# A second buffer for the gate's copy out of PSUM, and the decay exponentials with the token's own sum taken off by the matmul

## The chip, the cores and the metric

The kernel runs on one core of a Trainium2 chip. The metric is the device time of one execution in microseconds (us). The five engines of a core are named as in the profile: PE (TensorE, matmuls; PEld is its weight load), DVE (VectorE), ACT (ScalarE), POOL (GpSimd) and SP (SyncE, which here only issues DMAs).

## The reference

One layer of a bidirectional encoder in 32-bit floating point, on 1280 tokens (a prompt of 1024 and a sample of 256) of width 1024. A normed input is projected to three groups of heads that run side by side: six heads of a gated delta rule (DeltaNet) in both directions, six retention heads in both directions, and four heads of windowed attention. Each group's output is multiplied by a gate, and two dense stages follow. What the change touches, cut to its core:

```python
decay = jnp.cumsum(to_chunks(g, CHUNK), axis=-1)            # CHUNK = 64
gamma = jnp.exp(jnp.where(incl, decay[..., :, None] - decay[..., None, :], -jnp.inf))
a_mat = jnp.einsum('nbhcd,nbhsd->nbhcs', k_beta, k) * gamma
t_mat = jnp.where(strict, a_mat, 0.0) + jnp.eye(CHUNK, dtype=q.dtype)
sol = lax.linalg.triangular_solve(t_mat, rhs, left_side=True, lower=True, unit_diagonal=True)
qk = jnp.einsum('nbhcd,nbhsd->nbhcs', q, k) * gamma
...
o_a = (rms_norm(o_fwd + o_bwd, dn_norm_g) * jax.nn.silu(heads(a_gate, A_HEADS))).reshape(b, t, A_WIDTH)
o_b = head_layer_norm(r, ret_norm_g.astype(f32)) * jax.nn.silu(b_gate)
o_c = window_attention(...) * jax.nn.silu(c_gate)
```

`gamma` is the exponential of a difference of two running sums: that of the column's token and that of the row's own token. There is one 64x64 matrix of it per head, chunk and direction. `silu(gate)` is the gate times its sigmoid.

## The kernel before, in words

**Dense products.** Thirty products of the form "128 output columns times 1280 tokens" make up most of PE's work. To keep precision, weight and input are each split into a high and a low part, and a product is three matmuls for each of eight slices of the width, in three blocks of tokens (512, 512, 256). Their accumulators come from the PSUM tag "mm". Each block is then taken out of PSUM by an evacuation.

**Stages.** Input, norm and transposes come first; then nine products with a convolution each (34 to 213 us in the trace of before); among them `beta_alpha` (L317 to L371), which computes the running sums of the decays, writes their high and low parts to DRAM (`DRD`, L371, a POOL DMA) and keeps the negative of each token's own sum in `negd` (L364). Then comes `prep_stream` (L572 to L624; 213 to 345 us), woven with the ten products of `PP`: "cq0", "cq1", 6, 7, 3, "ck", "cv", 4, 0, 5. The products named by numbers are gates. After it come the second inversion, the attention, the scan over chunks (`join`, `step`), retention, and from about 850 us the two final dense stages. Products `PB` (gates 1 and 2, then "q0") run beside the attention.

**A gate's evacuation** (`evg`, L464 to L475): ACT copies the block out of PSUM into `zt` (tile "sz", L468); `sigmoid` makes `sg` from it with three activations (Exp L100, Ln L101, Exp L102); DVE multiplies `sg` by `zt`; for gates 0 to 5 an SP DMA writes the result to DRAM (`GD`, L472). `sz` and `sg` have one buffer each (SGB = 1). So a copy waits for the multiply of the block before, and L100 waits for the DMA of the block before.

**Preparing a block** (`prep_stream`): blocks of 128 tokens run from the last to the first, each in two directions d = 0, 1; one block in one direction is called a round here, 20 in all. Per block PE makes the grams ("sa") and transposes k into `kt` (PSUM tag "tr"), which ACT copies out (`kc`, L588). Per round POOL loads four rows of the running sums into DJ[d] (L591, two DMAs; one buffer per direction), PE makes two products `pd` of 128x384 (PSUM tag "sb") with DJ[d] as the moving and SD[0] or SD[1] as the stationary side, and ACT takes the exponential into `ge`: for the first `pd` six activations of 128x64 (L598), one for each head and chunk, because each has its own bias column of `negd`; for the second one of 128x384 (L601). The rows 64 to 127 of the first product bring in the mask. ACT then fills a column of `at` (L607; two buffers, AB = 2), DVE makes the products of grams and `ge` into `at` and `l2`, POOL copies `elc` (L616), and SP issues their DMAs (L618 to L621).

**Inversion and join.** `invert(1)` runs behind the fifth block, `invert(0)` behind the tenth: DVE inverts 32x32 pieces in steps, and the result goes through DRAM (`yd`, then `yn`) to `join`, whose matmuls on PE precede the scan.

**Order.** The generators are woven by due times written in the code (T_PREP and others), and a scheduler with a simulated timeline then sets each engine's order, with priority for weight splits and evacuations. Each engine works through its own list in order: what stands behind a waiting instruction waits too.

## Time and profile before

| what | value |
|---|---|
| median of 3 runs | 1095.5 us (1093.81 to 1100.48) |
| the profiled execution, its own time | 1098.55 us |
| its span | 1096.7 us |
| mean granted clock of PE in it | 0.959 |

The profile belongs to one execution, whose own time is 3.05 us above the median and 1.85 us above its span. Times inside it are microseconds from the start of the span. A line number behind an engine's name is that of the kernel before; a helper records all DVE products under L89 and all matmuls under L86, so that those are told apart by their tiles: `mm<-xh,whi` is a dense product, `sb<-dj,sd` a decay product, `sz` and `sg` are the gate's tiles, `ge` the exponentials, `at` and `l` what goes to the inversion and the scan.

### The profile page before, as it was taken

The numbers are of one execution on the slowest core, as the hardware profiler recorded it, in microseconds if no ns is written. First come the engines' busy times: TensorE is split into PE (matmuls) and PEld (weight loads), VectorE is DVE, ScalarE is ACT, GpSimd is POOL, SyncE is SP. The second block draws the span as 40 slices with busy tenths as digits, with TensorE's granted clock in tenths as the row PEclk, the third lists the DMA queues.
The fourth block names the chain that finished last, engine by engine and source line by source line (L and its number), as shares of the span: only waits on it lengthen the run. The fifth ranks groups of instructions, "written<-read, shape, count | busy, mean of one in ns | idle before, by whom it ended". The sixth has DMA issues, their size and how long they took to land.

```text
span 1096.7 us, 23201 instructions
## 1 busy us (share of the span) xinstructions
PE 1023.4 (93%) x8909; PEld 868.3 (79%) x8909; DVE 640.9 (58%) x1371; ACT 521.8 (48%) x1265; POOL 271.3 (25%) x430
## 2 busy tenths in 40 slices
PE   5999999999897889999998899999799999999996
PEld 4768878887775767878776777777579999999996
DVE  6666677477799679845565755575883123311125
ACT  7576776577456445344444322323342013455554
POOL 2001000022123021222233325544442211233421
PEclk9999999999999889999999799969889999999999
DMA  8112112367866363463464334554372432101003
GB/s 259 35 44 68 44 39 61 75 169 199 194 176 186 84 159 86 111 136 86 111 167 120 108 92 122 138 152 115 112 244 86 144 112 78 39 1 49 11 39 154
DMA packets 201415, 120.70 MB, mean 110 GB/s; under 512 B 105042, under 2 KB 186234, under 8 KB 201306
## 3 DMA queue, kind: packets, MB, share of 16 engines
q1 hardware_dynamic: 196410, 118.97, 39.8%
q8 instruction: 70, 1.15, 0.4%
q0 software_dynamic: 4896, 0.27, 0.4%
q14 instruction: 39, 0.32, 0.1%
HBM read 76.26 MB, written 42.91 MB: 109 GB/s over the span
## 4 chain that ended last, share of the span: by engine, by line
PE 63%; DVE 14%; DMA 10%; issue 4%; ACT 3%; SPq 2%; POOL 2%; DVEq 0%; ACTq 0%; POOLq 0%
PE mm L86 36%; PE sa L86 14%; PE sb L86 6%; PE tr L86 3%; DMA ad<-at 3%; DVE ot L89 3%; DVE l L89 1%; DMA yd<-ot 1%; SPq L618 1%; DMA gd<-sg 1%; DVE ot L966 1%; DMA vt<-vtd 1%; DMA yn<-yd 1%; DMA xt<-in_x_prompt 1%; PE tr L848 1%
## 5 line engine op out<-in xcount | busy, mean ns | idle before, releaser
L86 PE MATMUL mm<-xh,whi 128*128 128x512 f32 x720 | 270.0, 375 | 13.9 <-ACT sz L468 11.5
L86 PE MATMUL mm<-xl,whi 128*128 128x512 f32 x720 | 265.3, 369 | 0.0
L86 PE MATMUL mm<-xh,wlo 128*128 128x512 f32 x720 | 264.2, 367 | 0.0
L86 PEld LDWEIGHTS mm<-xh,whi 128*128 128x128 f32 x720 | 139.5, 194 | 40.0 <-ACT sz L468 13.5
L86 PEld LDWEIGHTS mm<-xh,wlo 128*128 128x128 f32 x720 | 139.6, 194 | 21.6 <-issue 0.5
L86 PEld LDWEIGHTS mm<-xl,whi 128*128 128x128 f32 x720 | 140.1, 195 | 20.5 <-issue 0.7
L89 DVE TENSOR_TENSOR ot<-ot 128x1284 f32<-128x1284 f32 (+16 forms) x131 | 88.0, 672 | 20.0 <-ACT ot L102 15.1
L86 PE MATMUL sa<-whi,xh 128*128 128x256 f32 x320 | 91.1, 285 | 0.0
L86 PE MATMUL sa<-whi,xl 128*128 128x256 f32 x320 | 90.4, 282 | 0.4 <-DVE xl L89 0.4
L86 PE MATMUL mm<-whi,xh 128*128 128x256 f32 x320 | 90.7, 284 | 0.0
L86 PE MATMUL mm<-whi,xl 128*128 128x256 f32 x320 | 90.4, 283 | 0.1
L86 PE MATMUL mm<-wlo,xh 128*128 128x256 f32 x320 | 90.3, 282 | 0.0
L86 PE MATMUL sa<-wlo,xh 128*128 128x256 f32 x320 | 90.1, 281 | 0.0
L89 DVE TENSOR_TENSOR sgm<-sb,sgm 128x256 f32<-128x256 f32 x40 | 17.0, 424 | 94.0 <-ACT sgm L102 73.8
L86 PEld LDWEIGHTS sa<-whi,xl 128*128 128x128 f32 x320 | 60.2, 188 | 0.8 <-DVE xl L89 0.6
L86 PEld LDWEIGHTS mm<-whi,xh 128*128 128x128 f32 x320 | 60.4, 189 | 0.4 <-issue 0.2
L86 PEld LDWEIGHTS sa<-whi,xh 128*128 128x128 f32 x320 | 60.2, 188 | 0.5 <-issue 0.3
L86 PEld LDWEIGHTS mm<-whi,xl 128*128 128x128 f32 x320 | 60.2, 188 | 0.5 <-DVE xl L89 0.3
L86 PEld LDWEIGHTS mm<-wlo,xh 128*128 128x128 f32 x320 | 60.3, 188 | 0.2 <-issue 0.2
L86 PEld LDWEIGHTS sa<-wlo,xh 128*128 128x128 f32 x320 | 60.2, 188 | 0.0
L525 DVE SCALAR_TENSOR_TENSOR ot<-ot,cols 128x1284 f32<-128x1284 f32 x36 | 55.9, 1552 | 0.6
L86 PE MATMUL sa<-sv,l 128*64 128x64 f32 (+1 forms) x912 | 47.3, 240 | 7.8 <-DVE sv L730 4.6
(294 smaller groups left out, 2097.3 us busy)
## 6 DMA issues: line engine op xcount, KB each, us to landing
raw<-in_w_in SPq DMA_DIRECT2D x28, 512.0 KB, 3.8
l2d<-l SPq DMA_DIRECT2D x20, 576.0 KB, 3.6
l<-l2d SPq DMA_DIRECT2D x40, 288.0 KB, 3.2
xt<-in_x_prompt SPq DMA_DIRECT2D x8, 512.0 KB, 6.9
x<-in_x_prompt SPq DMA_DIRECT2D x32, 128.0 KB, 2.7
raw<-in_w_pg SPq DMA_DIRECT2D x4, 1024.0 KB
yp<-ot SPq DMA_DIRECT2D x8, 512.0 KB, 2.7
ad<-at SPq DMA_DIRECT2D x20, 198.0 KB, 3.1
```

The lines of the kernel that those rows point to most:

```text
L86: nc.tensor.matmul(out, lhsT, rhs, start=start, stop=stop)
L89: eng.tensor_tensor(out=out, in0=a, in1=b, op=op)
L525: V.scalar_tensor_tensor(out=Y[:, 0:1284], in0=R[:, j:j + 1284], scalar=cw(ti, j), in1=Y[:, 0:1284], op0=MUL, op1=ADD)
L618: nc.sync.dma_start(out=AGD[d][b // 5][q, 2 * b % 10:2 * b % 10 + 2].rearrange("c p r x -> r (c p) x"), in_=at[32 * q:32 * q + 32, :, :, q ...
L848: nc.tensor.transpose(pt[:, k * 128:(k + 1) * 128], pr[:, k * 128:(k + 1) * 128], ident)
L966: V.scalar_tensor_tensor(out=st[r, b2, h], in0=st[r, b, h], scalar=gs[r, 2 * p + h:2 * p + h + 1], in1=kvt[r, b, h], op0=MUL, op1=ADD)
```

## The change

It has four parts.

1. `zt` ("sz") has two buffers; `sg` keeps one.
2. Small vectors give the room: `nea` is computed in place in `rvb`, `snk` lies in four columns of `rvb`, the attention's `mx`, `den` and `es` are slices of one tile `mde`, and `negd` is gone.
3. The token's own sum is taken off by the matmul. SD is now one stationary matrix per direction: its rows 4 to 27 are loaded in each round from a new DRAM tensor `NDD`, 24 rows of 128, by a third POOL DMA. DJ[d] has rows of ones there, written once by twelve POOL DMAs, each in the columns of its head and chunk. The first product then gives the difference itself, and one exponential of 128x384 stands in place of six of 128x64. The second product keeps a fixed stationary matrix, now named SO. `beta_alpha` writes the negated high and low parts to `NDD`: per direction one DVE operation of 60x512, two ACT copies and one POOL DMA more, and the DVE operation for `negd` less.
4. PSUM tags: `kt` moves from "tr" to "sb", and the first `pd` of a round from "sb" to "tr"; the second stays in "sb".

In the instructions' order this moves the following. First ACT, at the second run of gate products, beside the first attention blocks (`pts` are copies of the attention, `whi` a weight split). Before:

```order
L468 COPY sz_3645<-mm_3619 128x512
L149 CAST whi_3852<-raw_3850 128x1024
L850 COPY pts_3818<-tr_3815 128x256
L850 COPY pts_3824<-tr_3821 128x256
L100 ACTIVATE sg_3644<-sz_3645 128x512
L101 ACTIVATE sg_3644<-sg_3644,cols 128x512
L102 ACTIVATE sg_3644<-sg_3644 128x512
L468 COPY sz_3690<-mm_3664 128x256
L850 COPY pts_3836<-tr_3833 128x256
L100 ACTIVATE sg_3689<-sz_3690 128x256
```

The same gate blocks in the changed kernel:

```order
L475 COPY sz_3593<-mm_3567 128x512
L855 COPY pts_3763<-tr_3760 128x256
L855 COPY pts_3769<-tr_3766 128x256
L100 ACTIVATE sg_3547<-sz_3548 128x512
L855 COPY pts_3781<-tr_3778 128x256
L101 ACTIVATE sg_3547<-sg_3547,cols 128x512
L102 ACTIVATE sg_3547<-sg_3547 128x512
L855 COPY pts_3787<-tr_3784 128x256
L475 COPY sz_3638<-mm_3612 128x256
L100 ACTIVATE sg_3592<-sz_3593 128x512
```

The copy of a block (sz_3593) now stands ahead of the sigmoid of the block before it (sz_3548); before, each sigmoid followed its own copy.

Second POOL, in the first rounds of `prep_stream`, where it reloads the operands of the decay products. Before:

```order
L591 DMA dj_456<-drd_376 2x6x64 x2
L616 COPY elc<-ge_1961 128x6
L591 DMA dj_455<-drd_375 2x6x64 x2
L616 COPY elc<-ge_2049 128x6
L591 DMA dj_456<-drd_376 2x6x64 x2
L616 COPY elc<-ge_2108 128x6
```

The changed kernel there (dj_463 and dj_464 are DJ[0] and DJ[1], sd_327 and sd_328 are SD[0] and SD[1]):

```order
L601 DMA dj_464<-drd_382 2x6x64 x2
L622 COPY elc<-ge_1978 128x6
L602 DMA sd_327<-ndd_383 24x128
L601 DMA dj_463<-drd_381 2x6x64 x2
L622 COPY elc<-ge_2062 128x6
L602 DMA sd_328<-ndd_384 24x128
L601 DMA dj_464<-drd_382 2x6x64 x2
L622 COPY elc<-ge_2117 128x6
```

Each round has one DMA more on this queue, and it stands ahead of the reload of DJ and ahead of the next `elc`.

Third PE, at a round's two decay products (sd_326 and sd_327 of before are SD[0] and SD[1]). Before:

```order
L86 MATMUL mm_2411<-xl,whi_1994 128x256
L86 MATMUL sb_1903<-dj_455,sd_326 128x384
L86 MATMUL mm_2411<-xh,wlo_1995 128x256
L86 MATMUL sa_1877<-kq 64x128 x6
L86 MATMUL sa_1884<-kq 64x128 x6
L86 MATMUL sb_1911<-dj_455,sd_327 128x384
L584 MATMUL tr_2179<-ident,kq 128x128 x3
```

The changed kernel, at the second direction of the same block:

```order
L86 MATMUL mm_2287<-xh,wlo_2007 128x512
L86 MATMUL sa_1897<-kq 64x128 x6
L86 MATMUL sa_1904<-kq 64x128 x6
L86 MATMUL tr_1979<-dj_464,sd_328 128x384
L86 MATMUL sb_1982<-dj_464,so 128x384
L594 MATMUL sb_2050<-ident,kq 128x128 x3
L86 MATMUL mm_2399<-xh,whi_2006 128x256
```

The first decay product sits in a "tr" slot and waits for `sd` besides `dj`; the transposes of k sit in "sb". The products of the first five blocks lie closer together among the dense rows than before. Further on, the joins and the first scan steps stand earlier among the dense rows by up to about a product's length, until the two orders agree again.

The diff, cut to what is spoken of:

```diff
@@ -251,15 +251,16 @@
         sel(t2, onesbd, ALU.is_ge, 0.0, 0, 2 * d - 1, [[1 - 2 * d, 128]])
         MRbd.append(t2)
 
+
+    SO = pt_([128, 128], "so", F32R)
     SD = [pt_([128, 128], f"sd{i}", F32R) for i in range(2)]
-    for i in range(2):
-        V.tensor_scalar(out=SD[i], in0=ident, scalar1=0.0, scalar2=None, op0=MUL)
-        if i == 0:
-            for h in range(2):
-                S.copy(SD[i][64:128, 64 * h:64 * h + 64], ident[64:128, 64:128])
-        for l in range(2):
-            for h in range(2):
-                nc.gpsimd.dma_start(out=SD[i][2 * l + h:2 * l + h + 1], in_=onesbd[64 * (h ^ i):64 * (h ^ i) + 1])
+    for i, t in enumerate((*SD, SO)):
+        V.tensor_scalar(out=t, in0=ident, scalar1=0.0, scalar2=None, op0=MUL)
+        for h in range(2):
+            if i < 2:
+                S.copy(t[64:128, 64 * h:64 * h + 64], ident[64:128, 64:128])
+            for l in range(2):
+                nc.gpsimd.dma_start(out=t[2 * l + h:2 * l + h + 1], in_=onesbd[64 * (h ^ (i == 2)):64 * (h ^ (i == 2)) + 1])
 
 
     sumid = pt_([128, 24], "sumid")
@@ -296,8 +297,8 @@
     rvb = ct([128, 40], "rvb")
     V.tensor_copy(rvb, prv[:, 0:40])
     dtb, zb, sinkb = rvb[:, 12:24], rvb[:, 24:36], rvb[:, 36:40]
-    nea = ct([128, 12], "nea")
-    S.activation(out=nea, in_=rvb[:, 0:12], func=AF.Exp)
+    nea = rvb[:, 0:12]
+    S.activation(out=nea, in_=nea, func=AF.Exp)
     V.tensor_scalar(out=nea, in0=nea, scalar1=-1.0, scalar2=None, op0=MUL)
 
 
@@ -306,12 +307,13 @@
 
 
     sab = ct([128, 2, 2, NC, 3], "sab")
-    negd = ct([128, 2, NC, 3], "negd")
     nbeta = ct([128, 2, NC, 3], "nbeta")
     bed = ct([128, 2, NC, 3], "bed")
     elc = ct([128, 2, NC, 3], "elc")
 
     DRD = [tc.dram_tile([60, 2, 128], F32R, name=f"drd{d}") for d in range(2)]
+
+    NDD = [tc.dram_tile([60, 2, 2, 128], F32R, name=f"ndd{d}") for d in range(2)]
 
     def beta_alpha(pa):
 
@@ -361,7 +363,6 @@
             mm(pd[:, 0:60], MRbd[d], f(sab[:, 1, d]))
             S.activation(out=f(bed[:, d]), in_=pd[:, 0:60], func=AF.Exp)
             tt(V, bed[:, d], bed[:, d], sab[:, 0, d], MUL)
-            V.tensor_scalar(out=f(negd[:, d]), in0=pd[:, 0:60], scalar1=-1.0, scalar2=None, op0=MUL)
 
             pr = ps("tr")
             mm(pr[0:60, 0:128], f(sab[:, 1, d]), MRbd[d])
@@ -369,6 +370,12 @@
             S.copy(dr[:, 0], pr[0:60, 0:128])
             tt(V, dr[:, 1], pr[0:60, 0:128], dr[:, 0].bitcast(F32), SUB)
             nc.gpsimd.dma_start(out=DRD[d], in_=dr)
+            nd = pa.tile([60, 2, 2, 128], F32R, tag="l2", name=nm("nd"))
+            V.tensor_scalar(out=nd, in0=bc(ident[0:60].unsqueeze(1).unsqueeze(1), [60, 2, 2, 128]), scalar1=0.0, scalar2=None, op0=MUL)
+            for h in range(2):
+                hh = slice(64 * h, 64 * h + 64)
+                S.activation(out=nd[:, :, h, hh], in_=dr[:, :, hh].bitcast(F32), func=AF.Copy, scale=-1.0)
+            nc.gpsimd.dma_start(out=NDD[d], in_=nd)
 
 
     LKV = 768
@@ -464,7 +471,7 @@
             def evg(pp, t0, w):
                 o = ot[:, n, t0:t0 + w]
                 sg = o if n >= 6 else gp.tile([128, 512], F32, tag="sg", name=nm("sg"), bufs=SGB)[:, :w]
-                zt = gp.tile([128, 512], F32, tag="sz", name=nm("sz"), bufs=SGB)[:, :w]
+                zt = gp.tile([128, 512], F32, tag="sz", name=nm("sz"), bufs=2)[:, :w]
                 S.copy(zt, pp[:, :w])
                 sigmoid(sg, zt)
                 tt(V, sg, sg, zt, MUL)
@@ -503,6 +510,9 @@
             V.tensor_scalar(out=DJ[d][0:64], in0=bc(ident[0:64, 0:64].unsqueeze(1), [64, 6, 64]), scalar1=0.0, scalar2=None, op0=MUL)
             V.tensor_scalar(out=DJ[d][64:128], in0=bc(MRbd[d][64:128, 64:128].unsqueeze(1), [64, 6, 64]),
                             scalar1=-1.0, scalar2=1e30, op0=ADD, op1=MUL)
+
+            for n in range(6):
+                nc.gpsimd.dma_start(out=DJ[d][4 + 4 * n:8 + 4 * n, n, :], in_=onesR[0:4, 0:64])
         for z in range(2):
             for a0, a1 in ((0, 2), (1026, 1030), (1286, 1288)):
                 G.memset(ot[:, 3 * z, a0:a1], 0.0)
@@ -578,7 +588,7 @@
                         for h in range(2):
                             rw, o = slice(64 * h, 64 * h + 64), slice(64 - 64 * h, 128 - 64 * h)
                             mm(g3[r][o, p, :].rearrange("p (w t) -> p w t", w=2), kq[rw, p, 0, tk], kq[rw, p, :, tk])
-                kt = ps("tr")
+                kt = ps("sb")
                 kt3 = kt[:, 0:384].rearrange("p (q w) -> p q w", q=3)
                 for p in range(3):
                     nc.tensor.transpose(kt3[:, p, :], kq[:, p, 0, tb], ident)
@@ -589,16 +599,12 @@
                 for d in range(2):
                     for l in range(2):
                         nc.gpsimd.dma_start(out=DJ[d][2 * l:2 * l + 2], in_=DRD[d][6 * b:6 * b + 6, l].rearrange("n (s t) -> s n t", s=2))
+                    nc.gpsimd.dma_start(out=SD[d][4:28], in_=NDD[d][6 * b:6 * b + 6].rearrange("n l s t -> (n l s) t"))
                     ge = pa.tile([128, 2, 2, 3, 64], F32, tag="ge", name=nm("ge"))
                     for i in range(2):
-                        pd = ps("sb")
-                        mm(pd[:, 0:384], SD[i], DJ[d].rearrange("r n t -> r (n t)"))
-                        if i == 0:
-                            for n in range(6):
-                                S.activation(out=ge[:, 0, n // 3, n % 3], in_=pd[:, 64 * n:64 * n + 64], func=AF.Exp,
-                                             bias=negd[:, d, 2 * b + n // 3, n % 3:n % 3 + 1])
-                        else:
-                            S.activation(out=ge[:, 1].rearrange("p c q t -> p (c q t)"), in_=pd[:, 0:384], func=AF.Exp)
+                        pd = ps(("tr", "sb")[i])
+                        mm(pd[:, 0:384], (SD[d], SO)[i], DJ[d].rearrange("r n t -> r (n t)"))
+                        S.activation(out=ge[:, i].rearrange("p c q t -> p (c q t)"), in_=pd[:, 0:384], func=AF.Exp)
                     at = pa.tile([128, 2, 3, 2, 33], F32, tag="at", name=nm("at"), bufs=AB)
                     l2 = pa.tile([128, 2, 3, 3, 64], F32, tag="l2", name=nm("l2"))
                     last = 63 if d == 0 else 0
@@ -789,7 +795,7 @@
     V.scalar_tensor_tensor(out=bias, in0=bias, scalar=-1.0, in1=bias, op0=MUL, op1=ALU.min)
     sel(bias, bias, ALU.is_ge, -1e30, 0, -1, [[1, 384]])
     sel(bias, bias, ALU.is_ge, -1e30, 256, 1, [[-1, 384]])
-    snk = cb.tile([128, 4], F32, name="snk", bufs=1)
+    snk = rvb[:, 0:4]
     for h in range(4):
         V.tensor_scalar(out=snk[:, h:h + 1], in0=sinkb[:, h:h + 1], scalar1=1.0 / SLOPE[h], scalar2=None, op0=MUL)
 
@@ -813,9 +819,8 @@
             k0, k1 = max(b - 1, s0), min(b + 1, s1 - 1)
             nk = k1 - k0 + 1
             c0 = (k0 - b + 1) * 128
-            mx = cb.tile([128, 4], F32, tag="mx", name=nm("mx"))
-            den = cb.tile([128, 4], F32, tag="den", name=nm("den"))
-            es = cb.tile([128, 4], F32, tag="es", name=nm("es"))
+            mde = cb.tile([128, 12], F32, tag="mde", name=nm("mde"))
+            mx, den, es = (mde[:, 4 * i:4 * i + 4] for i in range(3))
             prs, pts = {}, {}
             qf = ot[:, 4:6, b * 128:(b + 1) * 128]
             qh = cb.tile([128, 4, 128], F32R, tag="qh", name=nm("qh"), bufs=QB)
```

## The prediction

> **What bounds the kernel now.** I read the page's head and its chain first, then the waits, then the windows from 100 to 392 us, then the timelines of TensorE and ScalarE at the places that those named.
>
> ```profile
> span 1096.7 us, 23201 instructions
> PE 1023.4 (93%) x8909; PEld 868.3 (79%) x8909; DVE 640.9 (58%) x1371; ACT 521.8 (48%) x1265; POOL 271.3 (25%) x430
> PE 63%; DVE 14%; DMA 10%; issue 4%; ACT 3%; SPq 2%; POOL 2%; DVEq 0%; ACTq 0%; POOLq 0%
> ```
>
> TensorE is busy for 93% of the span and carries 63% of the chain. The change leaves its matmuls as they are in number and size, so what can be won is idle or slow time of TensorE: 1096.7 - 1023.4 = 73 us stand idle, and busy time at a lowered clock comes on top. The waits that the change touches:
>
> ```profile
> POOL dj L591 <- PE sb L86: 40.8, 18, 5.2
> ...
> ACT sg L100 <- DMA gd<-sg: 32.8, 14, 6.2
> ...
> ACT at L607 <- DMA ad<-at: 17.8, 8, 4.6
> ...
> ACT sz L468 <- DVE sg L89: 15.9, 13, 5.9
> ...
> DVE at L89 <- ACT ge L598: 13.3, 8, 5.2
> ...
> PE mm L86 <- ACT sz L468: 11.5, 6, 3.9
> ```
>
> (Total, times, longest.) The copy of a gate block out of PSUM waits 13 times for the multiply that frees `sz`, and TensorE waits 6 times, 11.5 us, for that copy. ScalarE also stands before L100, which needs the one `sg` buffer back from its DMA, and before L607, which needs an `at` buffer back from its DMA. The windows (length, then busy time of TensorE, weight loads, VectorE, ScalarE, GpSimd, then the granted clock) show where TensorE loses:
>
> ```profile
> core 0: us, PE busy (x) PEld busy (x) DVE busy (x) ACT busy (x) POOL busy (x), PEclk, DMA share, GB/s
> 100.00:120.00 20.00, 19.98 (x106) 16.81 (x105) 11.98 (x12) 13.68 (x21) 2.84 (x6) 1.00 0.14 32
> 300.00:345.00 45.00, 42.58 (x267) 35.09 (x265) 43.02 (x93) 25.46 (x80) 8.23 (x17) 1.00 0.67 188
> 345.00:360.00 15.00, 5.05 (x31) 4.00 (x30) 14.45 (x29) 8.04 (x15) 8.11 (x14) 0.74 0.46 127
> 360.00:374.00 14.00, 14.00 (x52) 11.19 (x52) 12.04 (x40) 8.47 (x21) 0.79 (x2) 0.80 0.26 79
> 374.00:392.00 18.00, 14.09 (x73) 11.47 (x72) 5.37 (x8) 5.54 (x11) 0.11 (x1) 0.84 0.87 159
> ```
>
> From 300 to 360 us VectorE is nearly full (43.02 of 45, 14.45 of 15) and TensorE loses 10 of 15 us behind it; from 374 to 392 VectorE is nearly empty (5.37 of 18) and waits for the round trip of the inverses through DRAM.
>
> **Gate copies.** TensorE's longer waits for this copy, and the copies that end them:
>
> ```profile
> 279.65 0.50 PE L86 MATMUL mm<-xh,whi 128*128 128x512 f32 x1 [2.29 <-ACT sz L468]
> ...
> 359.70 0.79 PE L86 MATMUL mm<-xh,whi 128*128 128x512 f32 x1 [3.36 <-ACT sz L468]
> 360.29 0.63 PE L86 MATMUL mm<-xl,whi 128*128 128x512 f32 x1
> ...
> 365.41 0.55 PE L86 MATMUL mm<-xl,whi 128*128 128x512 f32 x1
> 365.80 0.39 PE L86 MATMUL mm<-xh,wlo 128*128 128x512 f32 x1
> ...
> 366.95 0.40 PE L86 MATMUL mm<-xl,whi 128*128 128x512 f32 x1
> ...
> 388.09 0.80 PE L86 MATMUL mm<-xh,whi 128*128 128x512 f32 x1 [3.91 <-ACT sz L468]
> 388.68 0.63 PE L86 MATMUL mm<-xl,whi 128*128 128x512 f32 x1
> ...
> 392.95 0.44 PE L86 MATMUL mm<-xh,wlo 128*128 128x512 f32 x1
> ```
>
> ```profile
> 278.99 0.21 ACT L607 COPY at<-nbeta 128x12 f32<-128x12 f32 x1 [4.65 <-DMA ad<-at]
> 279.22 0.37 ACT L468 COPY sz<-mm 128x256 f32<-128x256 f32 x1
> 279.49 1.34 ACT L598 ACTIVATE ge<-sb,negd 128x64 f32<-128x64 f32 x6
> 280.68 0.54 ACT L601 ACTIVATE ge<-sb 128x384 f32<-128x384 f32 x1
> ...
> 359.06 0.59 ACT L468 COPY sz<-mm 128x512 f32<-128x512 f32 x1 [5.89 <-DVE sg L89]
> ...
> 384.86 0.63 ACT L100 ACTIVATE sg<-sz 128x512 f32<-128x512 f32 x1 [6.16 <-DMA gd<-sg]
> ```
>
> The wait of 2.29 us at 279.65 is not one of `sz`: the copy came right behind L607, which had held ScalarE for 4.65 us. A second `sz` leaves it. At 359.70 and 388.09 the copy waited for `sz`, or stood behind a sigmoid that waited for `sg` while it held `sz`. With a second `sz` the copy goes ahead of that sigmoid, as the new order has it. These two are 3.36 + 3.91 = 7.27 us. What follows each also counts: after 359.70 the matmuls start (365.41 - 360.29) / 12 = 0.43 us apart, thirteen of them, and then (366.95 - 365.80) / 5 = 0.23. The granted clock of that window is 0.80. After 388.09 some twelve start 0.43 apart. That is 25 x 0.20 = 5.0 us. Together 12.3 us; the two smaller of the quoted six waits that are left would add 11.5 - 2.29 - 7.27 = 1.9, so the gain lies between nothing (TensorE waits at its next dependent row instead) and 14.2. I take 12: from 374 to 392 VectorE is no bound, and in 360 to 374 TensorE itself is.
>
> The Trainium skill, "TensorE: Matmul & The Clock Gate", part 1 on the clock gate, has half clock after an idle window of about 3.4 us and full clock again after about 3.4 us of work. That would make the slow stretches cost at most 1.7 us each, 3.4 together, and the sum would come out 1.6 us smaller in its gain. The rows disagree: the slow stretch behind 359.70 alone lasts to 365.80, six microseconds, and the trace decides.
>
> **Exponentials.** Rows of tile `ge` (lowest, median, highest ns; first and last start):
>
> ```profile
> L598 ACT ACTIVATE ge<-sb,negd x120: 295/324/362, 216.6 to 336.7; 128x64 f32<-128x64 f32 x120
> ...
> L601 ACT ACTIVATE ge<-sb x20: 468/523/553, 217.8 to 336.9; 128x384 f32<-128x384 f32 x20
> ```
>
> Six small ones take 1.34 us at 279.49, one wide one some 0.54: 0.8 us less in each of the 20 rounds. ScalarE's busy time is no bound there (25.46 of 45 us); what counts is VectorE, which waits 8 times, 13.3 us, for the last of the six. Each of these waits can shrink by 0.8, at most 6.4 us in all, since the larger part of them is L607's hold, which stays. What sets the pace of these rounds is told by the chain cut to 205 to 350 us:
>
> ```profile
> by line: DMA ad<-at 20.7%; PE mm L86 17.1%; DVE l L89 11.1%; SPq L618 10.4%; issue 6.6%; DVE ot L89 5.8%; DVE at L89 5.2%; DMA gd<-sg 4.4%; ACT ge L598 2.8%; DMA agd<-at 2.1%; PE sa L86 1.6%; DVE wlo L89 1.5%; DVE sg L89 1.3%; DVE kst L89 1
> ```
>
> L598 is 2.8% of 145 us, 4.1 us; of that 0.8 / 1.34 goes, 2.4 us, and `ad<-at` keeps its fifth. I take 3, between 0 (the ring of `at` gives the pace) and 6.4. This gain starts the first inversion earlier, and with it VectorE's full stretch.
>
> **The reload of the stationary rows.** Each round issues a third POOL DMA, 24 rows into SD[d]. Nearest row, and the landing of the tile that it belongs to:
>
> ```profile
> L591 POOL DMA_DIRECT2D dj<-drd x40: 546/548/598, 98.6 to 320.8; - x40
> ...
> DMA to landing us min/median/max: 1.7/3.1/5.7
> ```
>
> GpSimd gains 20 x 0.55 = 11 us of issue, hidden, as it is busy 8.23 of 45 us there. The DMA may start only when the matmul that reads SD[d] is done, and behind it on the queue wait `elc` and the other direction's reload. SD[d] is read once in two rounds: (336.9 - 217.8) / 19 = 6.3 us a round, 12.5 us between two reads. Three issues and a landing are 1.65 + 3.1 = 4.8 us, with the slowest landing 7.4. So it fits on the mean, with 5 to 8 us to spare, and GpSimd's own waits for TensorE (40.8 us in 18) show that it stood ready early. In the first blocks the new order sets the rounds closer. I take 2 us lost, between 0 and the 24 us of the last rival.
>
> **Edits at nothing.** PSUM slots: `kt` in "sb" and the first `pd` in "tr"; at most a slot is held through one L607 hold, 4.65 us, or freed as early; I take 0. In beta_alpha, per direction, one VectorE operation goes and one of 60x512 comes, two ScalarE copies and a POOL DMA; nearest rows:
>
> ```profile
> L364 DVE TENSOR_SCALAR negd<-tr x2: 213/213/213, 90.3 to 96.3; 128x60 f32<-128x60 f32 x2
> ...
> L369 ACT CAST dr<-tr x2: 248/254/261, 95.1 to 101.0; 60x128 fp32r<-60x128 f32 x2
> ```
>
> Some 1 us on each engine, beside TensorE at 19.98 of 20 us (window 100 to 120). On POOL the border MEMSET L523 stands behind the new DMAs; it comes 2 to 4 us later, and would cost that much if the convolution waited for it and TensorE for the convolution. The 12 set-up DMAs into DJ, 12 x 0.55 = 6.6 us, and the 4 for SO lie in a gap of POOL:
>
> ```profile
> 60.52 0.11 POOL L523 MEMSET ot<- 128x4 f32 x1 [52.06 <-ACT ot L531]
> ```
>
> It had waited 52 us. The small vectors that share a tile run the same instructions; a wait that this adds between blocks of attention has dense matmuls of TensorE beside it. I take 0 for both.
>
> **Sum.** -12 - 3 + 2 = -13 us. The profiled execution took 1098.55 us (span 1096.7, 1.85 around it), 3.05 above the median of 1095.5. 1098.55 - 13 = 1085.5, and less 3.05 gives 1082.5.
>
> **Rivals.**
>
> *sg still has one buffer.* L100 waits 32.8 us for its DMA, and that stays; the second `sz` lets one block more through, and the copy after it stands behind the sigmoid as now. For it: gate products 4, 0, 5 and then 1, 2 come as 15 blocks nearly in a row. Against: the long waits are two, not fifteen. Half of the first term is left: -6 - 3 + 2 = -7, 1088.5 us. Chance 0.17.
>
> *VectorE's chain absorbs it.* The joins and scan rows need inversion, DRAM trip and join:
>
> ```profile
> 374.36 9.66 DMA yd<-ot
> ```
>
> VectorE is 95% busy from 300 to 360. Where TensorE's copy waits go but this chain is not earlier, TensorE stands at the first join row, which the new order puts earlier among the dense rows, with dense work queued behind it. What is left is -3 + 2 or nothing: 1094 us. For it: the two full windows; against: TensorE runs out of work before VectorE only at 345 to 360. Chance 0.2.
>
> *Slower: the reload of SD lands late.* The queue behind L591 is GpSimd's, and `elc` on it waits for ScalarE. If the landing of 24 rows takes longer than 12 us from the matmul before, or the first ten rounds lie closer than 7.4 us to their direction's last, `pd` waits, with all dense matmuls queued behind it on TensorE, and the exponentials and VectorE behind that. At 4 us for six reloads, 24 us, it turns the gain: -13 - 2 + 24 = +9; with the clock falling behind each wait as after 359.70 (2.5 us), six times, +24: 1104 to 1120, say 1108. It decides from about 2 us late per round, or six times 4. Against it: 5 to 8 us of slack on the mean and landings of 5.7 at most, at a DMA share of 0.67 in the window from 300 to 345 us. Chance 0.13. The Trainium skill, "SBUF — State Buffer", the trap "DVE blocks DMA", says that a DMA issued from POOL finds its descriptors held up while VectorE runs an fp32 copy in a two-port mode; by that rule each added POOL DMA could come late in a full VectorE stretch. In this trace the 40 of L591 were issued in 546 to 598 ns beside VectorE at 43.02 of 45 us, which does not show it.
>
> **Chances.** Forecast 0.5, with an own range of 1074 (14.2 + 6.4 and no loss: 1098.55 - 20.6 - 3.05 = 1074.9) to 1090 (7.3, nothing, 2 lost). Over 1% is 11 us, under 1084.5 or over 1106.5; nearly that much is needed to tell this kernel's time from no change, whose three runs lie 6.7 us apart. The forecast lies two microseconds inside it: of its 0.5, and a little of the first rival, 0.45 is faster. Slower is the last rival's upper part and a shuffle of order, 0.12. The rest, 0.43, is within 1%. The range from 1070 to 1104 leaves out some 0.05 below and the slow rival, 0.13, above.
>
> **What would show it.** Right: `PE mm <- ACT sz` falls to the 2.3 us of L607's kind, the granted clock of 345 to 392 rises above 0.8, `ge` shows 40 rows of about 0.52 us, the chain's yd DMA starts 3 us or more before 374.36. Wrong: TensorE waits for `sd` or `dj` DMAs at the `tr` matmuls of 213 to 260 us, by over 2 us in more than a few; `PE mm <- ACT sz` is unchanged with `sg <- gd` as before; or TensorE's idle time from 213 to 464 us is as long and only has other names.

## The result and the profile after

The changed kernel takes 1105.12 us (median of 6 runs, 1103.24 to 1109.54), the kernel before 1095.74 beside it. The ratio is 1.0084, with a 95% interval of 1.0063 to 1.0105: some 9 us slower. The forecast was 1082.5, 13 us faster; the range reached to 1104. The profiled execution is the slowest of the six (1109.54), 4.4 us above their median, where that of before lies 3.05 above its own.

The page's head of the changed kernel, and its chain:

```profile
span 1107.8 us, 23154 instructions
...
PE 1035.1 (93%) x8909; PEld 874.2 (79%) x8909; DVE 640.7 (58%) x1372; ACT 507.0 (46%) x1171; POOL 298.6 (27%) x468
...
PE 68%; DVE 12%; DMA 9%; issue 4%; SPq 3%; ACT 3%; POOL 1%; DVEq 0%; POOLq 0%; ACTq 0%
```

ScalarE's 14.8 us less and GpSimd's 27 us more are there as the edit has them. The waits that the change aimed at, from the list of all waits of the changed kernel (total, times, longest):

```profile
ACT at L613 <- DMA ad<-at: 39.9, 12, 6.7
ACT sg L100 <- DMA gd<-sg: 31.8, 13, 8.7
...
POOL sd L602 <- PE sb L86: 29.6, 8, 12.7
...
ACT sz L475 <- DVE sg L89: 15.9, 7, 4.4
...
DVE ot L89 <- DMA ot<-agd: 8.9, 1, 8.9
...
PE mm L86 <- ACT sz L475: 4.4, 4, 2.1
```

TensorE's waits for the gate copy fell from 11.5 to 4.4 us. Of VectorE's 13.3 us of waits for the exponentials before its products into `at`, 1.2 are left. The copy's own wait for the multiply is 15.9 us as before, in 7 waits where it had 13. So the waits that the edits aimed at are shorter, and the time is longer all the same. Two other waits stand in the list: ScalarE's at the `at` copy rose from 17.8 to 39.9 us, and VectorE waits 8.9 us for `ot<-agd`, the operands of the first inversion.

Where the time went is seen when both traces are cut where TensorE has done the same amount of work (each matmul counted at the spacing that its shape has when it runs without a wait). The windows of the kernel before, and then of the changed kernel, at the same six cuts:

```profile
core 0: us, PE busy (x) PEld busy (x) DVE busy (x) ACT busy (x) POOL busy (x), PEclk, DMA share, GB/s
217.60:374.40 156.80, 140.20 (x839) 115.54 (x838) 132.92 (x299) 97.47 (x289) 35.13 (x73) 0.95 0.65 170
374.40:458.40 84.00, 77.61 (x855) 63.25 (x854) 66.43 (x131) 37.43 (x78) 16.29 (x15) 0.94 0.54 124
458.40:522.40 64.00, 61.31 (x728) 48.25 (x727) 36.50 (x114) 25.92 (x70) 12.41 (x22) 0.97 0.46 102
522.40:636.90 114.50, 104.54 (x1407) 81.51 (x1405) 70.23 (x224) 47.28 (x139) 36.09 (x78) 0.94 0.49 125
636.90:823.00 186.10, 173.36 (x1746) 135.19 (x1745) 122.50 (x296) 60.42 (x159) 86.48 (x123) 0.89 0.49 141
823.00:1096.70 273.70, 264.11 (x2235) 262.17 (x2233) 71.27 (x138) 106.75 (x269) 70.87 (x55) 0.99 0.21 71
```

```profile
core 0: us, PE busy (x) PEld busy (x) DVE busy (x) ACT busy (x) POOL busy (x), PEclk, DMA share, GB/s
218.70:369.50 150.80, 140.40 (x845) 115.66 (x844) 127.63 (x276) 77.55 (x180) 48.05 (x89) 0.97 0.66 177
369.50:464.20 94.70, 81.93 (x912) 67.00 (x910) 71.25 (x155) 41.70 (x91) 17.95 (x17) 0.91 0.49 112
464.20:538.80 74.60, 72.66 (x878) 55.29 (x878) 43.93 (x138) 32.33 (x85) 18.22 (x29) 0.91 0.50 115
538.80:642.50 103.70, 95.97 (x1149) 74.52 (x1148) 62.10 (x190) 39.88 (x118) 29.87 (x66) 0.95 0.44 112
642.50:830.60 188.10, 175.74 (x1794) 135.32 (x1793) 122.02 (x298) 61.08 (x161) 89.00 (x126) 0.90 0.51 143
830.60:1107.80 277.20, 266.51 (x2233) 264.54 (x2231) 71.29 (x138) 106.81 (x269) 70.67 (x55) 0.99 0.21 70
```

Up to the first cut the changed kernel is 1.1 us behind. Then:

| stretch of equal TensorE work | before, us | after, us | difference |
|---|---|---|---|
| preparation, gates, first inversion | 156.8 | 150.8 | -6.0 |
| first joins and attention blocks | 84.0 | 94.7 | +10.7 |
| attention, second inversion, scan | 64.0 | 74.6 | +10.6 |
| attention, scan | 114.5 | 103.7 | -10.8 |
| scan, retention | 186.1 | 188.1 | +2.0 |
| final dense stages to the end | 273.7 | 277.2 | +3.5 |

1.1 - 6.0 + 10.7 + 10.6 - 10.8 + 2.0 + 3.5 = 11.1, the difference of the spans. The stage that the change works on did become faster. The loss lies behind it, in code that the change hardly touches.

How far can this table be trusted? The third and the fourth stretch hold different numbers of matmuls in the two kernels (728 against 878, 1407 against 1149), and how the time divides between them depends on how small matmuls are counted; the three stretches from 374 to 637 us together are 10.5 us longer. Two traces of nearly the same order, before and `before_AB3` (below), lie 2 us apart at 374 us, 5 to 6 at the next three cuts and 11 at the end, although their medians agree within 0.1%. But the pattern comes again in six traces of the changed kernel, in its several orders: 1 to 5 us ahead of before at 374 us, 4 to 8 behind at 458, 2 to 10 behind at 637 us.

In the second and third stretch the granted clock is 0.91 where before has 0.94 and 0.97. What is missing from full clock there, (1 - clock) times the length, is 15.2 us against 7.0. So by this estimate up to 8 of the 21.3 us of these two stretches go with the lower clock.

From 369 to 410 us, at the first joins, TensorE of the changed kernel waits for the attention and the join; the same list of before, for the same time, had one entry, 3.9 us for the gate copy:

```profile
PE tr L86 <- ACT pts L855: 4.2, 2, 3.1
PE sb L86 <- DVE xn L670: 2.7, 1, 2.7
PE tr L853 <- DVE pr L850: 1.9, 1, 1.9
PE mm L86 <- ACT sz L475: 1.8, 1, 1.8
```

And the serial chain of inversion, DRAM and join does not come earlier. VectorE's timeline of before (a product of the round ahead; first instruction of the first inversion; its last one; first instruction of the second inversion; transposition for the first join; end of the second inversion):

```profile
280.25 0.36 DVE L89 TENSOR_TENSOR at<-sa,ge 128x192 f32<-128x192 f32 x1 [5.16 <-ACT ge L598]
...
283.89 4.08 DVE L89 TENSOR_TENSOR ot<-ot 120x2048 f32<-120x2048 f32 x1
...
373.14 0.11 DVE L424 MEMSET ot<- 120x64 f32 x1
...
390.16 3.96 DVE L89 TENSOR_TENSOR ot<-ot 120x2048 f32<-120x2048 f32 x1 [2.53 <-DMA ot<-agd]
394.24 0.67 DVE L664 STREAM_TRANSPOSE xn<-yn 128x480 f32<-128x480 f32 x1
...
463.45 0.11 DVE L424 MEMSET ot<- 120x64 f32 x1
```

and of the changed kernel (from the inversion's first instruction on):

```profile
278.70 4.04 DVE L89 TENSOR_TENSOR ot<-ot 120x2048 f32<-120x2048 f32 x1 [8.90 <-DMA ot<-agd]
...
372.19 0.11 DVE L431 MEMSET ot<- 120x64 f32 x1
...
392.05 3.95 DVE L89 TENSOR_TENSOR ot<-ot 120x2048 f32<-120x2048 f32 x1 [4.66 <-DMA yn<-yd]
...
395.92 0.68 DVE L670 STREAM_TRANSPOSE xn<-yn 128x480 f32<-128x480 f32 x1
...
474.09 0.11 DVE L431 MEMSET ot<- 120x64 f32 x1
```

The first inversion starts 5.2 us earlier, but ends only 1.0 earlier, the first join starts 1.7 later, and the second inversion ends 10.6 later. The earlier start is a matter of order. In before, the products of one more round (2 of `at`, 7 of `l`, from 280.25 on) stand ahead of the inversion on VectorE; in the changed kernel they stand behind it, so that 20 and 70 are ahead where there were 22 and 77. The work was moved and not saved: from 217 to 374 us VectorE is busy for 133.1 us before and 133.4 after.

### The profile page after: what moved, and what is told of

Same layout as the page of the kernel before. It is cut to its first block, busy times and chain, and to the rows that moved or that the text cites. A ratio compares the mean times of both kernels' runs of the same rounds, so it can differ in the third digit from the quotient of the medians.

```text
span 1107.8 us, 23154 instructions
## 1 busy us (share of the span) xinstructions
PE 1035.1 (93%) x8909; PEld 874.2 (79%) x8909; DVE 640.7 (58%) x1372; ACT 507.0 (46%) x1171; POOL 298.6 (27%) x468
## 4 chain that ended last, share of the span: by engine, by line
PE 68%; DVE 12%; DMA 9%; issue 4%; SPq 3%; ACT 3%; POOL 1%; DVEq 0%; POOLq 0%; ACTq 0%
PE mm L86 37%; PE sa L86 15%; PE sb L86 7%; PE tr L86 4%; DVE ot L89 2%; DVE l L89 2%; DMA agd<-at 2%; PE tr L853 1%; SPq L624 1%; DMA yn<-yd 1%; DMA xt<-in_x_prompt 1%; DVE ot L971 1%; DMA ad<-at 1%; DMA gd<-sg 1%; PE tr L1164 1%
## 5 line engine op out<-in xcount | busy, mean ns | idle before, releaser
L89 DVE TENSOR_TENSOR sgm<-sb,sgm 128x256 f32<-128x256 f32 x40 | 17.0, 424 | 94.7 <-ACT sgm L102 74.3
L89 POOL TENSOR_TENSOR wlo<-raw,whi 128x2048 fp32r<-128x2048 f32 x7 | 32.3, 4610 | 90.8 <-ACT whi L1079 90.8
```

The source lines that it names most:

```text
L89: eng.tensor_tensor(out=out, in0=a, in1=b, op=op)
```

## The experiments

Each is timed in three rounds beside the kernel before. Ratios are to the kernel before, with the 95% interval.

**First, the parts one by one.** The theories were: the loss is in the gate part (copies run ahead, sigmoids and multiplies come late); it is in the PSUM slots; or it is in the order, dealt out anew by the scheduler whatever the edit.

`room_only`: only the small vectors.

```diff
-    nea = ct([128, 12], "nea")
+    nea = rvb[:, 0:12]
-    snk = cb.tile([128, 4], F32, name="snk", bufs=1)
+    snk = rvb[:, 0:4]
-            mx = cb.tile(...); den = cb.tile(...); es = cb.tile(...)
+            mde = cb.tile([128, 12], F32, tag="mde", name=nm("mde"))
```

> The kernel before with the small vectors shared (nea, snk and mx/den/es as in the change) and nothing else. Order theory: the loss of the change comes from the list of instructions being dealt out anew in the middle of the kernel, and this edit, which by itself costs nothing, deals it out anew too: a ratio to before that is clear of 1 by 0.3 to 1%, in either direction, with TensorE's waits for the gate copy still near 11 us. Gate theory and slot theory: nothing moves, ratio within 0.2% of 1.

Measured: 1.0102 (1.0064 to 1.0140). TensorE's waits for the gate copy are 10.2 us.

`sz_only`: the small vectors, and the second `sz` buffer; `negd` lies in the preparation's pool, for room.

```diff
-                zt = gp.tile([128, 512], F32, tag="sz", name=nm("sz"), bufs=SGB)[:, :w]
+                zt = gp.tile([128, 512], F32, tag="sz", name=nm("sz"), bufs=2)[:, :w]
```

> The kernel before with the second sz buffer and the small vectors shared (the negated sums lie in the pool of the preparation instead, for room); the exponentials and PSUM tags stay. Gate theory (letting copies run ahead of the sigmoids makes sigmoids and gate multiplies late, and the attention and joins behind them): 0.7 to 1.2% slower than before, like the whole change, the gate multiplies around 375 us some 10 us later. My forecast's first term: 1% faster, TensorE's waits for the copy down from 11.5 to some 4 us. Order theory: it lies where the room-only kernel lies, within 0.5%.

Measured: 1.0124 (1.0090 to 1.0157). The waits for the gate copy are still 9.5 us.

`tag_only`:

```diff
-                kt = ps("tr")
+                kt = ps("sb")
-                        pd = ps("sb")
+                        pd = ps(("tr", "sb")[i])
```

> The kernel before with the PSUM tags swapped alone (kt in sb, the first decay product in tr). Slot theory (transposes of k and decay products now wait for each other's slots): 0.5 to 1% slower, with the rounds of the preparation some 5 us behind at 290 us. Order theory: any ratio from 0.99 to 1.01, and the preparation ends at the same time within 2 us. Gate theory: within 0.2%.

Measured: 1.0089 (1.0055 to 1.0122).

`no_second_sz`: the changed kernel with `bufs=SGB` for `sz`.

> The changed kernel with one sz buffer again; all else as changed. Gate theory: back to the time of before or better, ratio 0.995 to 1.000. Forecast's first term: slower than the changed kernel by 1%, ratio 1.015 to 1.02. Order theory: anything from 0.99 to 1.015, not tied to the gate waits. Slot theory: as slow as the changed kernel, 1.008.

Measured: 1.0095 (1.0062 to 1.0128); waits for the gate copy 8.0 us.

All four lie within 0.4% of each other and about 1% above before. `tag_only` shares no edit with `room_only` and `sz_only`; the other three share the small vectors. That speaks for something that any edit sets off, such as the order, and the two explanations from the parts (gate and slots) don't cover all four. But `tag_only` doesn't refute the slots: its loss is not in the middle. Counted as in the table above, it is already 9 us behind before at 374 us, in the preparation that its edit touches, with 15.7 us of waits for the gate copy.

`tag_only` also tells what the exponentials do not do. It keeps all six, and yet VectorE's wait for them is nearly gone and its first inversion starts where that of the changed kernel does, with the same wait:

```profile
DVE at L89 <- ACT ge L598: 1.5, 3, 1.1
...
278.68 3.96 DVE L89 TENSOR_TENSOR ot<-ot 120x2048 f32<-120x2048 f32 x1 [9.13 <-DMA ot<-agd]
```

**Second, the order by itself.**

`order_only`: no instruction is added or removed.

```diff
-T_JOIN, T_AT, OF, HV = 5.0, 5.4, 6, ()
+T_JOIN, T_AT, OF, HV = 5.0, 5.39, 6, ()
```

> The kernel before with one number of its order changed: the due time of an attention block, T_AT, is 5.39 where it was 5.4. The instructions are the same; TensorE's list differs from its row 1987 on, the middle of the kernel (joins, attention, scan). Order theory, which the first four runs favour (every edit came out about 1% slower): clear of 1 by at least 0.4%, slower more likely than faster, since the order of before lies well by chance or choice, with the loss behind 380 us. Theories that put the loss into the parts of the change (gate, slots): 1.000 within 0.2%.

Measured: 1.0084 (1.0055 to 1.0114), as much as the whole change. Its runs spread widely, 1101.06 to 1113.71, and the profiled execution was the fastest of them, so its trace shows less than the ratio: 2.6 us between the spans. Cut at equal TensorE work, one stretch is longer, from 523 to 646 us, 123.1 us where before has 114.5, and the next one gives 6.8 back:

```profile
456.90:523.00 66.10, 63.12 (x686) 49.04 (x685) 36.53 (x115) 26.80 (x73) 10.58 (x21) 0.97 0.43 97
523.00:646.10 123.10, 109.48 (x1492) 84.86 (x1491) 71.15 (x224) 46.64 (x139) 39.95 (x82) 0.90 0.48 123
646.10:825.40 179.30, 167.77 (x1699) 130.06 (x1698) 122.01 (x294) 60.20 (x157) 87.53 (x120) 0.92 0.50 142
```

`room_same_order`: the small vectors without `snk`, and `negd` in the preparation's pool. With `snk` left alone TensorE's, GpSimd's and SyncE's lists are those of before.

```diff
-    negd = ct([128, 2, NC, 3], "negd")
+        negd = pa.tile([128, 2, NC, 3], F32, name="negd", bufs=1)
```

> The kernel before with nea in place, the attention's small vectors in one tile and the negated sums in the preparation's pool, but snk in a tile of its own: here TensorE's, GpSimd's and SyncE's lists stay as they were, word for word. Order theory: 1.000 within 0.3%, although it shares the small vectors as the room-only kernel did (1.010). Theory that sharing the small vectors costs time by waits in the attention: 1.010 again.

Measured: 1.0025 (1.0002 to 1.0047). From `room_only`'s 1.0102 it differs by the places of `snk` and `negd`. The move of `negd` is in `room_same_order` and left TensorE's list as it was, so the likely cause of the step is the new order that follows when one vector of four columns (`snk`) lies in another tile. The 0.25% that is left is met again below.

`sz_near_order`: `room_same_order` and the second `sz` buffer.

> The room_same_order kernel plus the second sz buffer. Its lists differ from those of before less than any other kernel with two sz buffers (TensorE's from row 969 on). Forecast's first term: 0.5 to 1.1% faster than before, 213 to 374 us shorter by 4 to 6 us and the gain kept. Order theory: the gain of 4 to 6 us up to 374 us is there, and what stands at the end is decided behind it, anywhere from 0.993 to 1.012. Gate theory (sigmoids late): 1.008 to 1.012.

Measured: 1.0124 (1.0080 to 1.0169). At equal TensorE work:

```profile
217.80:372.50 154.70, 140.93 (x842) 116.16 (x841) 124.10 (x272) 93.60 (x278) 33.80 (x72) 0.96 0.68 171
372.50:457.00 84.50, 75.56 (x699) 60.37 (x699) 64.11 (x129) 36.90 (x76) 11.24 (x10) 0.94 0.46 105
457.00:538.80 81.80, 70.81 (x955) 55.79 (x949) 49.33 (x150) 34.32 (x88) 16.86 (x29) 0.90 0.48 107
```

The ratio lies just above the order theory's range. The first stretch gains 2.1 us, less than the 4 to 6 that were expected, and the third, the attention beside the second inversion, loses 17.8 (81.8 for 64.0), though it holds more matmuls than in before (955 for 728). The first inversion ends at 383.1 us, where `room_same_order` has 373.9. TensorE's waits for the gate copy are 11.9 us, against 14.3 in `room_same_order`.

`change_own_snk`: the changed kernel with `snk` in its own tile.

> The changed kernel whole, but snk in a tile of its own as before: the same work and waits, another order. Order theory: differs from the changed kernel's 1.0084 by at least 0.3% in either direction. Theory that the change's parts carry the loss: 1.0084 within 0.2%.

Measured: 1.0119 (1.0076 to 1.0162). Its interval overlaps that of the changed kernel, so by itself it decides nothing; it is one more order of the change.

**Third, more orders of both kernels, and the exponentials alone.** `before_T56`, `change_T56` and `change_T52` change only T_AT, to 5.6, 5.6 and 5.2.

> The kernel before with T_AT 5.6: the same instructions in a second other order (TensorE's list differs from row 1935 on). Order theory: slower than before by 0.4 to 1.2%, as order_only's 1.008, since before's own order is the good one among its neighbours. Rival: order_only was a single bad draw, and this one lies within 0.3% of 1.

Measured: 1.0032 (1.0010 to 1.0054), less than the 0.4% that was expected and a little more than its rival's 0.3%.

> The changed kernel with T_AT 5.6. Order theory: 1.004 to 1.014, no better than before with the same number. Forecast's rival (the change does gain, and only its one order is bad): at least 0.5% faster than before_T56.

Measured: 1.0148 (1.0116 to 1.0180), just above the range.

> The changed kernel with T_AT 5.2, a third order of it (before with 5.2 has almost the list of order_only, 1.0084). Order theory: 1.004 to 1.014. If the change gains by itself: below 1.004.

Measured: 1.0108 (1.0082 to 1.0133).

So the first theory was too simple. The orders of before lie at 1.000, 1.003 and 1.008, those of the change at 1.008, 1.011, 1.012 and 1.015. That suggests a loss of the change's own on top of the order, and doesn't show it: the kernels with nothing but small vectors moved lie at 1.0025 and 1.0102, and T_AT 5.4 may have been picked because it is fast in before.

`exp_only`: the changed kernel with the PSUM tags of before and one `sz` buffer, so that the exponentials, the loaded rows and the small vectors are left.

> The own sums taken off by the loaded rows and one exponential for six, with the PSUM tags of before and one sz buffer. Reload rival (the 24 rows land late): TensorE's decay products wait for their DMA by over 1 us in more than five rounds, 213 to 300 us longer by 10 us, 1.01 or more. Forecast's second and third terms: the first inversion starts 3 us or more before 283.9 us, no wait for sd; the end by order, 0.998 to 1.012.

Measured: 1.0166 (1.0141 to 1.0191), the slowest of all. The reload rival's sign is absent: no wait of TensorE for `sd` or `dj`. What TensorE waits for, from 205 to 400 us:

```profile
PE mm L86 <- ACT sz L475: 8.9, 6, 3.6
PE sb L86 <- ACT ge L607: 7.4, 5, 2.1
```

The 7.4 us (1.3 before) are "sb" slots that an exponential still holds. ScalarE's wait at the `at` copy is 42.9 us. The first inversion starts at 281.4 us, 2.5 us earlier and not the 3 that were expected, and ends at 378.3, 5.2 later than in before. At the cut at 374 us this kernel is 2.5 us behind before, so the exponentials show no gain where they were to give 3 us. Its ratio lies above the 1.012 that was expected without waits for the reload.

**Fourth, the ring of `at`.** The wait at the `at` copy rises with the exponentials: from 17.8 us in before (18 to 30 in the kernels that keep its six) to 31 to 45 us in those with one for six. `tag_only`'s 29.5 with six lies close to `no_second_sz`'s 30.8 with one. The theory was that this ring takes up what they save. A third buffer should take the wait away.

```diff
-AB = 2
+AB = 3
```

> The changed kernel with three at buffers instead of two (AB = 3). Theory that the ring of at takes the saved exponentials' time (ScalarE's wait at the at copy for its DMA rose from 17.8 to 39.9 us): that wait falls below 15 us, the first inversion starts at 275 us or earlier, and the whole is faster than the changed kernel by at least 0.4%, below 1.004 of before. Order theory: the wait falls, but the end stays at 1.004 to 1.015. Theory that the added loads (24 rows a round) cost: waits of the preparation unchanged.

Measured: 1.0060 (1.0035 to 1.0085).

> The kernel before with three at buffers. Ring theory: the wait of 17.8 us at the at copy falls below 8, a gain of at most 5 us up to 374 us, since the ring bound less here; the end by order, 0.995 to 1.010.

Measured: 0.9997 (0.9967 to 1.0027).

> The exp_only kernel (1.0166) with three at buffers. Ring theory: 1.007 or less, the wait at the at copy from 42.9 to below 15 us and TensorE's 7.4 us of waits for ge gone. Order theory: 1.004 to 1.017 with the wait gone all the same.

Measured: 1.0129 (1.0104 to 1.0154).

> The changed kernel with three at buffers and T_AT 5.2, a second order of it. Ring theory: below change_T52's 1.0108 by at least 0.4%. Order theory: 1.004 to 1.015, not tied to the ring.

Measured: 1.0077 (1.0048 to 1.0107).

A third buffer leaves TensorE's matmuls in the order that they had, but for a few in before and in `change_T52`, so that these four nearly compare one order with itself. The times come down by 0.03% in before and by 0.2 to 0.4% in the others, within the intervals, but the wait did not go: 21.4 us in `before_AB3`, 36.4 in `change_AB3`, 44.1 in `exp_only_AB3`, 40.2 in `change_AB3_T52`. So the ring theory, which wanted these waits below 8 or 15 us and a gain of 0.4% or more, fell. In the trace the copy only runs one round further ahead and stands there as long. The wait shows ScalarE ahead of the rounds, and it says nothing of what sets their pace.

**Fifth, the tag swap beside the exponentials.** `no_tag_swap` is the changed kernel with the tags of before; `exp_only_T56` is `exp_only` with T_AT 5.6.

> The changed kernel with the PSUM tags of before (kt in tr, both decay products in sb). It fills the grid of parts: exponentials alone 1.0166, with the tag swap 1.0095, all parts 1.0084. If the tag swap is what makes the exponentials bearable (it takes away TensorE's 7.4 us of waits for sb slots held by ge): 1.012 to 1.018 with those waits back. If order decides: 1.004 to 1.018, not tied to those waits.

Measured: 1.0119 (1.0079 to 1.0160), with 4.3 us of TensorE's waits for "sb" slots held by `ge`.

> The exp_only kernel with T_AT 5.6, another order. If exp_only's 1.0166 is its own: 1.013 to 1.020, TensorE's waits for ge on sb slots again 5 us or more. If it was a bad draw of the order: 1.004 to 1.012.

Measured: 1.0138 (1.0109 to 1.0167), with 6.5 us of such waits.

The second of these was hardly a new order: T_AT 5.6 leaves the first 5757 of TensorE's 8909 matmuls as they were in `exp_only`, and nine tenths of what follows, so that it repeats the number more than it tests it. That `exp_only` has a bad order thus isn't excluded. With the tag swap the waits for those slots fall to 0.7 us in the changed kernel, and the ratios are 1.0095 (`no_second_sz`) and 1.0084. The swap points the right way beside the exponentials, and the wrong way in before (`tag_only`, 1.0089). `exp_only` and `no_second_sz` differ by it alone, and their intervals lie apart; those of `no_tag_swap` and the changed kernel overlap. What it is worth apart from the order these runs do not settle.

**The second buffer, in pairs.** Four pairs of these kernels differ by the second `sz` buffer (in the second pair `negd` lies elsewhere too). How much earlier or later TensorE has done the same work with two buffers than with one, from the traces, counted as above:

| one buffer, two buffers | at 374 us of before | at 637 us | ratios |
|---|---|---|---|
| `no_second_sz`, changed kernel | 9.7 us earlier | 3 earlier | 1.0095, 1.0084 |
| `room_only`, `sz_only` | 3.9 earlier | 5 later | 1.0102, 1.0124 |
| `room_same_order`, `sz_near_order` | 2.9 earlier | 13 later | 1.0025, 1.0124 |
| `exp_only`, `no_tag_swap` | 4.5 earlier | 4 earlier | 1.0166, 1.0119 |

Between two traces of nearly one order the first of these numbers differs by up to 2.3 us and the second by up to 6. So the second buffer gives 3 to 10 us up to 374 us, in every pair, though in two of them not by much more than that spread; nothing of one sign is left at 637 us. The gain comes by the order too. In before TensorE has no dense row from 349.0 to 359.7 us and mostly stands, and the gate copy is only the end of it:

```profile
355.54 0.80 PE L86 MATMUL sb<-kst,qlz 128*128 128x256 f32 x2 [5.10 <-DVE qlz L89]
```

This row of the attention waits for VectorE. In all kernels with two buffers one or two blocks more of a dense product stand ahead of it (1416 dense matmuls, for 1368 or 1392), and they fill part of the stand: from 345 to 360 us TensorE of the changed kernel is busy for 11.41 us, where before has 5.05.

No version was found that clearly beats the kernel before.

## Why the prediction was wrong

**The steps that failed.** Two steps carry the sum to the end of the kernel. The first is that TensorE's gain at the gate copies stays, "from 374 to 392 VectorE is no bound, and in 360 to 374 TensorE itself is". The second is that the exponentials' gain "starts the first inversion earlier, and with it VectorE's full stretch". Both failed. What the second buffer gave at 374 us, 3 to 10 us in the four pairs, has no one sign left at 637. The full stretch ended 1.0 us earlier, the first join started 1.7 us later, and behind the 6.0 us that were gained up to 374 us the next three stretches lose 10.5. The last of the prediction's own signs of being wrong came true: from 213 to 464 us TensorE is idle for 23.0 us before and 23.2 after, under other names. Two signs of being right came as well (40 rows of `ge` of about 0.49 us; a granted clock of 0.89 for 0.79 from 345 to 392 us), and so they told of the stage alone.

**The kernel's bound.** Read rightly for the stretch up to 374 us. There TensorE's idle time fell from 16.6 to 10.4 us (156.80 - 140.20 and 150.80 - 140.40), and the stretch is 6.0 us shorter, of the 15 in the forecast's first two terms.

**The gate term, -12.** Right in kind up to 374 us, and mis-sized: the pairs show 3 to 10 us there for the second buffer. The names of the waits don't show it: from one buffer to two the waits for the gate copy go from 10.2 to 9.5 us, from 14.3 to 11.9, from 8.0 to 4.4, and from 11.7 up to 14.1, while they are 11.5 and 16.0 in before and `before_AB3`, two traces of nearly one order. The price of 3.36 us at 359.70 took the end of a stand of 10 us for the whole. The rival that `sg` keeps one buffer was right in its wait: `sg` still waits 31.8 us for its DMA.

**The clock in that term, 5.0 us.** The rows were read rightly, but the judgement of the rule was hasty. The granted clock of before, around the restart at 359.70:

```profile
359.00:363.00 4.00, 3.30 (x8) 2.62 (x9) 3.87 (x13) 1.68 (x5) 0.00 (x0) 0.50 0.73 197
363.00:366.00 3.00, 3.00 (x9) 2.34 (x8) 1.90 (x4) 1.98 (x3) 0.00 (x0) 0.55 0.00 0
366.00:376.00 10.00, 10.00 (x54) 8.48 (x53) 8.86 (x31) 6.42 (x16) 0.79 (x2) 1.00 0.19 52
```

Half clock lasts until shortly before 366, 6 us after the restart. The Trainium skill, "TensorE: Matmul & The Clock Gate", part 1, also says that the window of some 3.4 us runs freely. By that page's figure a restart inside a window would stay slow for the rest of it and for one whole window more, up to 6.8 us, an estimate; the trace agrees with that here, with its 6 us. The prediction took the rule for 3.4 us after every restart and called the rows a contradiction, which they are not.

**The exponentials, -3.** No run shows this gain. `exp_only` is 2.5 us behind before at 374 us, and its inversion ends 5.2 us later. That the first inversion of the changed kernel starts 5.2 us earlier, more than forecast, is no proof of the term: `tag_only` has the same start with six exponentials. VectorE had waited 13.3 us for `ge`; now it waits 8.9 us for `ot<-agd`, because the inversion, moved ahead of a round's products, has to read back what was just written. The question "what is late next" was not asked here.

**The reload, +2.** Right in kind. No wait of TensorE for `sd` or `dj` shows in the changed kernel, so that the 2 us are not seen either. Its rows (lowest, median, highest ns; landings in us):

```profile
L602 POOL DMA_DIRECT2D sd<-ndd x20: 537/540/545, 100.8 to 323.2; - x20
...
DMA to landing us min/median/max: 1.8/3.5/5.8
```

That is the duration and the landing estimated from L591. The slower rival with its chance of 0.13 had the right sign by a mechanism that did not occur. The rule of the Trainium skill that was weighed beside it ("SBUF — State Buffer", the trap "DVE blocks DMA") is not seen in these rows either: four of the twenty were issued from 300 to 345 us, where VectorE is busy for 43.65 of 45 us, in 537 to 545 ns like the rest. That VectorE ran in a two-port mode there no run shows, so this doesn't test the rule.

**Edits at nothing.** The small vectors were costed at 0. `room_same_order` is 1.0025 with an interval just above 1, 2.7 us; the final stages show where (last section). The 1.1 us at the first cut aren't those of set-up and `beta_alpha` alone: `exp_only`, which has both, stands there with before. The PSUM slots, taken at 0 as well, are not nothing: `tag_only` is 9 us behind before at 374 us.

**VectorE's chain absorbs it.** This rival, at 0.2, is the part of the story that the traces bear out best: the join starts at a time set by inversion and DRAM, TensorE reaches it with less dense work left, and stands in the attention (4.2 us), at the join (2.7) and at `pr` (1.9). But its price of 1094 supposed that the loss ends at the gain. It didn't: the three stretches from 369.5 to 642.5 us lose 10.5 us together, where 6.0 had been gained.

**What no case priced: the order itself.** Every term was a wait taken away in an order held fixed, with the old middle behind it. The chances name "a shuffle of order", inside the 0.12 for slower, without a time. The scheduler dealt out the middle anew, and that alone is worth two thirds of the 13 us of the forecast: 0.8%, some 9 us, for T_AT 5.39 in place of 5.4, with the same instructions, and as much between `room_same_order` and `room_only`. The range was therefore too narrow on the slow side. The new order was there to be read; the prediction saw the joins stand earlier among the dense rows, and used it for one rival only.

**What stays open.** At the same or nearly the same T_AT and number of `at` buffers the change is slower each time: 1.0084 to 1 (5.4), 1.0108 to 1.0084 (5.2 and 5.39, within the intervals), 1.0148 to 1.0032 (5.6), 1.0060 to 0.9997 (three `at` buffers), 0.72% on the mean or 8 us. Of this some 0.25% goes with the small vectors; exponentials that hold "sb" slots while ScalarE stands elsewhere may have a share. The rest was not traced to one wait, and how it divides between order and change is open. As the change and the kernel before never ran in one and the same order, an order of the changed kernel that keeps its 6 us can't be excluded. Holding the order of before while the second buffer or the exponentials are put in was not tried.

## What to carry to other kernels

Where a scheduler lists the instructions, make a change of no cost first (a due time altered by 0.2%, a vector moved), and measure how far that alone carries the time: here 0.3 to 1%, as much as the gains that were argued for. A stall that goes is worth what its next serial step gives: follow it to the read-back, the DRAM trip and the join, and count the gain where the last of these starts. And compare the two traces at equal work of the busiest engine, not at equal times: then a gain in one stage and a loss behind it are seen as two things. Do it for two traces of one order first (here they lie up to 11 us apart at the end), and for a part that can be added to several kernels do it in pairs: that showed the second buffer's gain, which the names of the waits had hidden.

## What the hardware showed beside this

Matmuls of the final dense stages run at slightly different spacings. From 960 to 1020 us TensorE is busy throughout at full clock in all kernels, and the number of matmuls in these 60 us (behind the x) differs, whatever the DMA's share beside them (the figure behind the clock). Before, and then `tag_only`:

```profile
960.00:1020.00 60.00, 60.00 (x509) 1.00 0.07 23
```

```profile
960.00:1020.00 60.00, 60.00 (x509) 1.00 0.13 40
```

and `room_same_order`, and then the changed kernel:

```profile
960.00:1020.00 60.00, 60.00 (x505) 1.00 0.07 23
```

```profile
960.00:1020.00 60.00, 60.00 (x505) 1.00 0.12 40
```

The median spacing from 850 us on is 117 ns in the five kernels that keep the small vectors as they were (before, `tag_only`, `order_only`, `before_T56`, `before_AB3`), and 120 ns in all others but `room_only`, which has 118. The mean spacing is 117.8 to 118.2 ns in the five and 119.1 to 120.0 in the others, some 2 to 5 us over the 2233 matmuls of the stage. It goes with the edit of the small vectors, not with the order. That the operands lie at other addresses in SBUF then is a guess; no run moved them alone.
